# The decay and beta projection of a decoder step as an fp32 product on four column groups

## The chip, the cores and the metric

The kernel runs on one core of a Trainium2 chip. Time is device time in microseconds for one execution of the whole step. TensorE (PE in the profile) multiplies, VectorE (DVE), ScalarE (ACT) and GpSimd (POOL) work element by element, and SyncE (SP) issues the transfers.

## The reference, cut to what matters

One layer of a hybrid decoder is computed for a prompt of 512 tokens and for 8 x 4 sample tokens, 544 columns in all. The front of the layer is an input projection of a shifted and scaled x:

```
shift, scale, gate = split(silu(c) @ w_cond + b_cond, 3)
h = x * (1 + scale) + shift
[qa, ka, va, za, qkv_b, zb, a_b, b_b, g_a, g_b] = h @ w_in
```

Scale and shift have one value per feature for the whole prompt, and one per feature for each of the 8 sample rows. The change touches only a_b and b_b, 8 + 8 output columns of the 11280. From them come the decay exp(-exp(A_log) * softplus(a + dt_bias)) and beta = sigmoid(b) of the gated delta rule. Everything behind (attention, delta rule, gates, output projection, layer norm) stays as it is.

## The kernel before, in words

The 1024 input features are 8 k-tiles of 128. All activations lie with features on partitions, and a product has 544 columns in two halves of 272 (HF). Most products are made of three fp32r products of a high and a low part of each operand.

The kernel doesn't issue its instructions as it writes them down. `body` records them, and `schedule` works out one order for all engines: it plays the recording through with an estimated duration for each instruction, and on each engine takes the ready one with the smallest (rank, number), number being the place in the recording. Rank -1 goes first, the front's work has 0, the long stream of projections 9, the cache moves 30. The moves have due times spread over the planned run. PSUM banks are handed out in the recorded order within a rank: `pg` has three banks, `pp` and `pd` two, `pb` one. `rec.together()` keeps a group of instructions in one piece. `rec.either` lets the order choose ACT or DVE for an evacuation.

The front (up to about 52 us) needs c first. `cond_block(1, ...)` makes the scale and `cond_block(0, ...)` the shift, in blocks of one or two k-tiles, with products on four column groups: k-tile k goes to the output partitions 32 (k mod 4) and on, and a product with the 0/1 matrix `selc` then adds the four groups and turns the result. The blocks use a bank of `pg` or of `pb` in turn. To keep TensorE at work while the shift is not yet known, the first three projection tiles (`sums`, of W3) are computed from x1 = x * scale, in high and low parts `x1[0]` and `x1[1]`, and the part of the shift is added afterwards, as sh @ W3. The sums hold two banks each of `pp`, `pd` and `pg`. When the shift is there, h is written over x in `xT`, and `hhi` and `hlo` are its parts for the stream of projections.

The 16 columns of a_b and b_b lie behind the other 384 in W3. Before, their high and low parts stand side by side as the 32 columns of `hl`, and 2 halves x 8 k-tiles x 2 parts of x1 = 32 products give `abT`, with the high part in rows 0 to 15 and the low part in rows 16 to 31. Two ACT copies evacuate it. The shift's part is added to rows 0 to 15. In `gates()`, products with the 0/1 matrices `sel16` and `selab`, which repeat every 16 rows, add the rows that belong together and put tokens on partitions; decay and beta follow from there.

Of the kernel before, what the change touches and what calls it, by code (L numbers as in the profile page):

```python
# [11 lines left out]
F32 = mybir.dt.float32  # L12
F32R = mybir.dt.float32r
AF = mybir.ActivationFunctionType
# [6 lines left out]
KT = 8  # L21
SEQ = 512
# [3 lines left out]
NT = SEQ + NS  # L26
HF = NT // 2
# [223 lines left out]
class Recorder:  # L251
# [21 lines left out]
    def pool(self, make, name, bufs, side):  # L273
        return Pool(self, make, name, bufs, side)
# [506 lines left out]
def body(ctx, tc, io):  # L781
    rec = Recorder()
    pe, ve, se, ge, sp = rec.engines()
# [19 lines left out]
    def pg():  # L803
        return psg.tile([128, 512], F32, name="pg", tag="g")
# [4 lines left out]
    def pb_():  # L809
        return psb.tile([128, 512], F32, name="pb", tag="b")  # L810
# [14 lines left out]
    def C(name, where="early"):  # L825
        a, n = CCOLS[name]
        return tables[where][:, a:a + n]
# [13 lines left out]
    op = pool(octx, "opool", 9, "right")  # L841
# [41 lines left out]
    xT = fx.tile([128, KT, NT], F32, name="xT")  # L883
    W3 = fx.tile([128, KT, 400], F32, name="W3")
    sc = fx.tile([128, KT, 9], F32, name="sc")
    sh = fx.tile([128, KT, 32], F32, name="sh")
    early_ = op.tile([128, NT], F32, name="cg", tag="o")
    n = CONST[2].shape[1]
# [1 line left out]
    dta = early_[:, n:n + 68].rearrange("p (a b) -> p a b", b=34)  # L890
    shifts = early_[:, n + 68:n + 104].rearrange("p (a b) -> p a b", b=9)
    first = [op.tile([128, NT], F32, name="raw", tag="o") for _ in range(3)]
    abT = op.tile([128, NT], F32, name="abT", tag="o")[0:32]
    xs = xT[:, :, SEQ:].rearrange("p k (b t) -> p k b t", t=4)
    per_token = lambda t, k, n: t[:, k:k + n, 1:9, None].to_broadcast([128, n, 8, 4])
    cols_of = lambda n: slice(n * HF, (n + 1) * HF)
    with ExitStack() as fctx:
        fr = pool(fctx, "front", 1)
# [27 lines left out]
        sp.dma_start(bnw, io["b_norm_w"])  # L926
        ve.memset(cs, 0.0)
        ge.memset(sh, 0.0)
        th = fr.tile([128, KT, 9], F32, name="th")
        se.activation(th, cT, AF.Tanh, scale=0.5)  # L930
        ve.tensor_scalar(th, th, 0.5, 0.5, op0=OP.mult, op1=OP.add)
# [2 lines left out]
        def cond_block(part, at, m, other):  # L934

            ps, wc, w = pb_() if other else pg(), pieces[part, at], 128 * m
            idle = IDLE if (part, at) == (1, 0) else (0, 0, 0)
            rec.rank = -1

            def turn_over(n):  # L940
                for _ in range(n):
                    pe.matmul(ps[:, 384:512], ones, ones, start=True, stop=True)

            turn_over(idle[0])
            with rec.together():
                for k in range(KT):
                    q = k % 4
                    pe.matmul(ps[32 * q:32 * q + 32, 0:w].rearrange("p (a b) -> p a b", b=128), cs[:, k, :], wc[:, :, k, :],
                              start=(k < 4), stop=(k >= 4), tile_position=(0, 32 * q)).at = 9.9 * ((part, at) == (1, 1))
                turn_over(idle[1])  # L950
            Y = fr.tile([128, 256], F32, name="Y", bufs=2)
            ve.tensor_copy(Y[:, 0:w], ps[:, 0:w])
            pv = ps[:, 256:256 + 16 * m].rearrange("p (a b) -> p a b", b=16)
            with rec.together():
                for i in range(m):
                    pe.matmul(pv[:, i, 0:9], Y[:, 128 * i:128 * i + 128], C("selc", "first"), start=True, stop=True)
                turn_over(idle[2])
            rec.rank = 0
            return pv[:, :, 0:9], bT[:, 8 * part + at:8 * part + at + m, None].to_broadcast([128, m, 9])

        x1 = [fr.tile([128, KT, NT], F32R, name=f"x1{u}") for u in "hl"]
        sums = [[f()[:, :HF] for _ in range(2)] for f in (pp, pd, pg)]
        for b, (c, m) in enumerate(CHUNKS):
            pv, bias = cond_block(1, c, m, b % 2)
            kk = slice(c, c + m)
            ve.scalar_tensor_tensor(sc[:, kk], pv, 1.0, bias, op0=OP.add, op1=OP.add)
            for k in range(c, c + m):
                se.activation(x1[0][:, k, :SEQ], xT[:, k, :SEQ], AF.Copy, scale=sc[:, k, 0:1])
                if k == c:
                    ve.tensor_mul(xs[:, kk], xs[:, kk], per_token(sc, c, m))  # L970
                    se.activation(x1[0][:, kk, SEQ:], xT[:, kk, SEQ:], AF.Copy)
                    ve.tensor_sub(x1[1][:, kk, SEQ:], xT[:, kk, SEQ:], x1[0][:, kk, SEQ:].bitcast(F32))
                ve.scalar_tensor_tensor(x1[1][:, k, :SEQ], xT[:, k, :SEQ], sc[:, k, 0:1], x1[0][:, k, :SEQ].bitcast(F32),
                                        op0=OP.mult, op1=OP.subtract)
            hi, lo = (wsp.tile([128, D], F32R, name=n, tag=n)[:, 0:384 * m].rearrange("p (k c) -> p k c", k=m) for n in ("hi", "lo"))
            se.activation(hi, W3[:, kk, 0:384], AF.Copy)
            ve.tensor_sub(lo, W3[:, kk, 0:384], hi.bitcast(F32))
            for k in range(c, c + m):
                for t in range(3):
                    w, w_ = (x[:, k - c, 128 * t:128 * t + 128] for x in (hi, lo))  # L980
                    for n in range(2):
                        for a, x in ((w, 0), (w, 1), (w_, 0)):
                            pe.matmul(sums[t][n], a, x1[x][:, k, cols_of(n)], start=(k == 0 and a is w and x == 0),
                                      stop=(k == KT - 1 and a is w_))
        for t in range(3):
            for n in range(2):
                rec.either(first[t][:, cols_of(n)], sums[t][n])
        hl = fr.tile([128, KT, 32], F32R, name="hl")
        se.activation(hl[:, :, 0:16], W3[:, :, 384:400], AF.Copy)
        ve.tensor_sub(hl[:, :, 16:32], W3[:, :, 384:400], hl[:, :, 0:16].bitcast(F32))  # L990
        ps = [pg(), pg()]
        for n in range(2):
            for k in range(KT):
                for x in range(2):
                    pe.matmul(ps[n][0:32, :HF], hl[:, k], x1[x][:, k, cols_of(n)],
                              start=(k == 0 and x == 0), stop=(k == KT - 1 and x == 1))
        for n in range(2):
            se.activation(abT[:, cols_of(n)], ps[n][0:32, :HF], AF.Copy)
        for c, m in two_by_two:
            pv, bias = cond_block(0, c, m, c % 4)  # L1000
            kk = slice(c, c + m)
# [2 lines left out]
        ps, pv = pg(), pb_()  # L1004
        with rec.together():
            for k in range(KT):
                q = k % 4
                pe.matmul(ps[32 * q:32 * q + 32, 0:400], sh[:, k, :], W3[:, k, :], start=(k < 4), stop=(k >= 4),
                          tile_position=(0, 32 * q))
# [113 lines left out]
    def gates():  # L1123
# [14 lines left out]

        pa = pg()
        for c in range(4):  # L1140
            pe.matmul(pa[:, c * 16:c * 16 + 16], abT[:, c * 128:(c + 1) * 128], C("sel16", "g")[0:32], start=True, stop=True)
        sab = C("selab", "g").rearrange("p (a b) -> p a b", b=4)
        for h4 in range(4):
            pe.matmul(pa[32 * h4:32 * h4 + 32, 64:68], abT[:, SEQ:], sab[0:32, h4, :], start=True, stop=True)
        zero = op.tile([128, NT], F32, name="zero", tag="o")[0:16, 0:512]
        ge.memset(zero, 0.0)
        ab = d1.tile([128, 2, 34], F32, name="ab")
# [36 lines left out]
        g = d1.tile([128, 34], F32, name="g")  # L1184
# [356 lines left out]
    pairs = [{} for _ in range(4)]  # L1541
# [637 lines left out]
    rules = threads.add(chain(delta_rule), 0)  # L2179
    blocks = threads.add(chain(delta_blocks), 1)  # L2180
    threads.add(gates(), -2)
    threads.add(stream(57 + 4 + EARLY_B), 9)
    ap = pool(actx, "ap", 1)
# [125 lines left out]
    for k in range(0, KT, 2):  # L2309
        name = ("hi", "lo")[k // 4]  # L2310
# [69 lines left out]
    for tt, n in ((0, 0), (1, 0), (2, 0), (None, 0), (0, 1), (1, 1), (2, 1), (3, 0), (3, 1)):  # L2380
# [3 lines left out]
        q = r[tt]  # L2384
        step = 256 if n and tt == 3 else 512
        for c in range(512 * n, 512 * n + 512, step):
            po = product_out(tt, c, c + step)
            w = slice(c, c + step)
# [129 lines left out]
```

## Time and profile before

| | |
|---|---|
| median of 3 runs | 880.43 us (878.79 to 882.06) |
| profiled execution | 878.32 us, its span 876.5 us |
| granted TensorE clock, mean | 0.997 |
| busy: PE, DVE, ACT, POOL | 859.6, 643.1, 451.2, 69.6 us |
| chain that ended last | PE 84%, DVE 5%, ACT 4%, DMA 4% |
| DMA | 236.18 MB, mean 269 GB/s |

The span goes from the first to the last instruction of the core. PE counts matmuls, PEld weight loads, which run beside them. A row of the timeline has start and length in us, engine, line, operation, out<-in with the names of the tiles, the array's shape (rows*columns), the moving operand and the number of instructions merged; in brackets stands how long the engine was idle before it and what released it. All lines are L728, since one helper issues everything, so rows are told apart by tile names. An fp32 product is two records of the trace, an fp32r product one. The ends of matmuls are modelled; distances of starts are used below.

### The profile page before, as it was taken

To read this page: it belongs to the slowest core of one execution; us is meant where nothing else is said; L and a number is where in the kernel's file an instruction comes from. 1 tells how busy PE (TensorE), PEld (TensorE's weight loads), DVE (VectorE), ACT (ScalarE), POOL (GpSimd) and SP (SyncE) were. 2 spreads that over 40 slices of the span, in tenths; PEclk is the share of its full clock that TensorE was granted. 3 is DMA by queue.
4 is the path that set the end of the run, shared out by engine and by line. 5 is a ranking of instruction groups with operands and counts; after the bars stand their busy time and mean duration, and the time that the engine had idled before them with its cause. 6 is when DMAs were issued, how large, how long until landed. Compare 5 with 4: busy or idle time off the path is not lost.

```text
span 876.5 us, 20668 instructions
## 1 busy us (share of the span) xinstructions
PE 859.6 (98%) x8152; PEld 811.5 (93%) x8152; DVE 643.1 (73%) x1328; ACT 451.2 (51%) x1069; POOL 69.6 (8%) x167
## 2 busy tenths in 40 slices
PE   8999999999999999999999999999999999999996
PEld 7889999898999899999999998999999999999875
DVE  4775557565448999967999853556999699998547
ACT  3546656765546786447785446732442213234442
POOL 0120110110001110001020000011010000001000
PEclk9999999999999999999999999999999999999998
DMA  9976769666697886999877896469969899986984
GB/s 334 348 216 201 234 204 284 239 198 223 189 268 237 286 278 201 289 281 311 306 218 263 259 289 210 160 216 307 356 213 373 277 409 420 372 314 205 351 290 147
DMA packets 120493, 236.18 MB, mean 269 GB/s; under 512 B 49110, under 2 KB 76576, under 8 KB 117708
## 3 DMA queue, kind: packets, MB, share of 16 engines
q1 hardware_dynamic: 120396, 234.86, 80.0%
q8 instruction: 64, 1.05, 0.5%
q14 instruction: 33, 0.27, 0.1%
HBM read 218.53 MB, written 103.97 MB: 368 GB/s over the span
## 4 chain that ended last, share of the span: by engine, by line
PE 84%; DVE 5%; ACT 4%; DMA 4%; issue 1%; SPq 1%; POOL 0%; DVEq 0%; ACTq 0%
PE pp L728 64%; PE pg L728 9%; PE pd L728 8%; PE pb L728 4%; ACT L728 1%; DMA slab<-in_ks 1%; DMA dO<-orow 1%; DMA wc<-in_w_cb 1%; DMA wv<-dw 1%; DVE slab L728 1%; ACT sq L728 1%; DVE acc L728 1%; ACT hi L728 1%; DVE lo L728 1%; SPq L728 1%
## 5 line engine op out<-in xcount | busy, mean ns | idle before, releaser
L728 PE MATMUL pp<-hhi,hi 128*128 128x272 f32 x1360 | 397.6, 292 | 2.1 <-DVE zt L728 1.4
L728 PE MATMUL pp<-hhi,lo 128*128 128x272 f32 x1360 | 397.3, 292 | 0.0
L728 PE MATMUL pp<-hlo,hi 128*128 128x272 f32 x1360 | 395.7, 291 | 0.0
L728 PEld LDWEIGHTS pp<-hhi,hi 128*128 128x128 f32 x1360 | 256.4, 188 | 5.0 <-issue 1.8
L728 PEld LDWEIGHTS pp<-hhi,lo 128*128 128x128 f32 x1360 | 256.4, 188 | 2.1 <-issue 1.4
L728 PEld LDWEIGHTS pp<-hlo,hi 128*128 128x128 f32 x1360 | 256.3, 188 | 1.4 <-issue 0.4
L728 ACT ACTIVATE hi<-wt 128x1024 fp32r<-128x1024 f32 (+1 forms) x101 | 103.5, 1025 | 170.4 <-PE pp L728 141.2
L728 DVE TENSOR_TENSOR lo<-wt,hi 128x1024 fp32r<-128x1024 f32 (+1 forms) x101 | 118.9, 1177 | 71.6 <-ACT hi L728 71.3
L728 DVE SCALAR_TENSOR_TENSOR acc<-ext,cw,acc 128x568 f32<-128x568 f32 x72 | 58.0, 805 | 1.6 <-ACT acc L728 0.6
L728 DVE TENSOR_TENSOR slab<-slab 128x512 f32<-128x512 f32 (+1 forms) x66 | 42.9, 667 | 7.0 <-DMA slab<-in_vs 4.1
L728 DVE TENSOR_REDUCE slab<-slab 128x8 f32<-128x512 f32 (+2 forms) x66 | 42.7, 658 | 3.3 <-ACT slab L728 2.9
L728 ACT ACT_TABLE_LOAD x32 | 41.1, 1283 | 4.2 <-DMA dO<-orow 1.7
L728 ACT ACTIVATE zt<-pp 128x272 f32<-128x272 f32 x48 | 18.7, 389 | 37.7 <-PE pp L728 36.3
L728 PE MATMUL pp<-ybh,lo 128*128 128x272 f32 x128 | 36.9, 288 | 0.0
L728 PE MATMUL pp<-ybh,hi 128*128 128x272 f32 x128 | 36.9, 288 | 0.0
L728 ACT ACTIVATE P<-P,st 128x256 f32<-128x256 f32 (+1 forms) x64 | 31.1, 487 | 11.1 <-DVE st L728 11.0
L728 PE MATMUL pp<-ybl,hi 128*128 128x272 f32 x128 | 36.8, 287 | 0.0
L728 POOL COPY cx<-ext 128x3 f32<-128x3 f32 (+1 forms) x48 | 21.7, 480 | 151.4 <-ACT ext L728 149.9
L728 DVE CUSTOM_DVE_ANT_0 P<-pg,bias 128x256 f32<-128x256 f32 (+1 forms) x64 | 23.1, 403 | 13.2 <-PE pg L728 13.1
L728 PEld LDWEIGHTS pp<-ybh,hi 128*128 128x128 f32 x128 | 24.2, 189 | 0.2
L728 ACT ACTIVATE spare<-pp 128x272 f32<-128x272 f32 (+1 forms) x32 | 16.3, 509 | 15.5 <-PE pp L728 15.5
L728 PEld LDWEIGHTS pp<-ybh,lo 128*128 128x128 f32 x128 | 24.1, 189 | 0.1
(421 smaller groups left out, 1539.5 us busy)
## 6 DMA issues: line engine op xcount, KB each, us to landing
out_kv_s<-in_cache SPq DMA_DIRECT2D x144, 512.0 KB
wt<-in_w_in SPq DMA_DIRECT2D x85, 512.0 KB
out_kv_s<-in_cache SPq DMA_DIRECT2D x24, 496.0 KB
wc<-in_w_cb SPq DMA_DIRECT2D x16, 512.0 KB
slab<-in_ks SPq DMA_DIRECT2D x32, 256.0 KB
slab<-in_vs SPq DMA_DIRECT2D x32, 256.0 KB
kv<-in_ks SPq DMA_DIRECT2D x16, 512.0 KB
kv<-in_vs SPq DMA_DIRECT2D x16, 512.0 KB
```

The costliest lines, as they stand in the source:

```text
L728: getattr(real[x.engine], x.name)(*map(arg, x.args), **{k: arg(v) for k, v in x.kw.items()})
```

## The change

The products for a_b and b_b become plain fp32 products on four column groups. `wab` has the 16 weight columns and 16 columns of zeros for each k-tile. For the prompt, `wsc` is wab times the prompt's scale, and the moving operand is the raw x: 8 products of 512 columns, recorded with rank -1 and ahead of the evacuation of the sums. For the sample tokens, whose scales differ, 16 products of 32 columns take wab with the two parts of x1, read as fp32. `abT` now has 128 rows, four partial sums of 32 rows, and the selecting products run over 128 rows in place of 32, and add the four.

```diff
-    abT = op.tile([128, NT], F32, name="abT", tag="o")[0:32]
+    abT = op.tile([128, NT], F32, name="abT", tag="o")
...
+        wab, wsc = (fr.tile([128, KT, 32], F32, name=name) for name in ("wab", "wsc"))
+        ge.memset(wab, 0.0)
...
+        se.activation(wab[:, :, 0:16], W3[:, :, 384:400], AF.Copy)
+        ve.tensor_mul(wsc, wab, sc[:, :, 0:1].to_broadcast([128, KT, 32]))
+
+        def ab_product(out, pairs):
+            with rec.together():
+                for i, (w, x) in enumerate(pairs):
+                    q = 32 * (i % 4)
+                    pe.matmul(out[q:q + 32], w, x, start=(i < 4), stop=(i >= len(pairs) - 4), tile_position=(0, q))
+
+        ps = pg()
+        rec.rank = -1
+        ab_product(ps, [(wsc[:, k], xT[:, k, :SEQ]) for k in range(KT)])
+        se.activation(abT[:, :SEQ], ps, AF.Copy)
+        rec.rank = 0
         for t in range(3):
             for n in range(2):
                 rec.either(first[t][:, cols_of(n)], sums[t][n])
-        hl = fr.tile([128, KT, 32], F32R, name="hl")
-        se.activation(hl[:, :, 0:16], W3[:, :, 384:400], AF.Copy)
-        ve.tensor_sub(hl[:, :, 16:32], W3[:, :, 384:400], hl[:, :, 0:16].bitcast(F32))
-        ps = [pg(), pg()]
-        for n in range(2):
-            for k in range(KT):
-                for x in range(2):
-                    pe.matmul(ps[n][0:32, :HF], hl[:, k], x1[x][:, k, cols_of(n)],
-                              start=(k == 0 and x == 0), stop=(k == KT - 1 and x == 1))
-        for n in range(2):
-            se.activation(abT[:, cols_of(n)], ps[n][0:32, :HF], AF.Copy)
+        ps = pg()[:, 0:32]
+        ab_product(ps, [(wab[:, k], x1[x][:, k, SEQ:].bitcast(F32)) for k in range(KT) for x in range(2)])
+        se.activation(abT[:, SEQ:], ps, AF.Copy)
...
-            pe.matmul(pa[:, c * 16:c * 16 + 16], abT[:, c * 128:(c + 1) * 128], C("sel16", "g")[0:32], start=True, stop=True)
+            pe.matmul(pa[:, c * 16:c * 16 + 16], abT[:, c * 128:(c + 1) * 128], C("sel16", "g"), start=True, stop=True)
...
-            pe.matmul(pa[32 * h4:32 * h4 + 32, 64:68], abT[:, SEQ:], sab[0:32, h4, :], start=True, stop=True)
+            pe.matmul(pa[32 * h4:32 * h4 + 32, 64:68], abT[:, SEQ:], sab[:, h4, :], start=True, stop=True)
```

## Prediction

> **What bounds the kernel now.** First the page: its span, then the busy share of each engine.
>
> ```profile
> span 876.5 us, 20668 instructions
> PE 859.6 (98%) x8152; PEld 811.5 (93%) x8152; DVE 643.1 (73%) x1328; ACT 451.2 (51%) x1069; POOL 69.6 (8%) x167
> ```
>
> TensorE is busy nearly all the time, but a busy TensorE need not be one that sets the end, so the next view is the table by stretches (length, then busy time and instruction count of each engine, granted clock, DMA share).
>
> ```profile
> 0.00:13.00 13.00, 9.99 (x84) 8.74 (x85) 4.67 (x18) 4.28 (x8) 0.52 (x5) 1.00 0.82 280
> 13.00:30.00 17.00, 16.95 (x153) 14.65 (x153) 9.85 (x23) 6.97 (x13) 0.00 (x0) 1.00 1.03 412
> 30.00:39.00 9.00, 9.00 (x95) 6.87 (x94) 5.81 (x15) 4.32 (x9) 1.95 (x3) 1.00 1.01 398
> 39.00:48.60 9.60, 9.60 (x90) 6.87 (x89) 6.75 (x15) 5.79 (x12) 4.74 (x10) 1.00 0.74 170
> 76.00:200.00 124.00, 123.97 (x1222) 117.94 (x1222) 75.04 (x179) 77.10 (x193) 14.32 (x43) 1.00 0.73 237
> 200.00:850.00 650.00, 644.52 (x6192) 614.48 (x6191) 501.04 (x979) 326.37 (x770) 45.03 (x93) 1.00 0.83 278
> ```
>
> The reader is to see three things. From 13 to 48.6 us, where the whole change lies, TensorE has 0.05 us without work, at a granted clock of 1.00. From 76 to 200 us it has 0.03 us without work, so whatever TensorE is spared before 48 us is handed on. In the 650 us after that it lacks 5.48 us, the only stretch in which small waits could swallow or return anything. So the change is worth the TensorE time that it takes away or adds, as long as TensorE always has something else to run in its place.
>
> **What is removed.** The 32 products of x1 with the narrow weights. Rows of the tile hl (duration ns, first and last start), and the first and the last of twelve such products in a row on the timeline:
>
> ```profile
> L728 PE MATMUL pg<-x1h,hl x16: 282/287/289, 40.2 to 47.6; 128*32 128x272 f32 x16
> L728 PE MATMUL pg<-x1l,hl x16: 282/287/314, 40.3 to 47.7; 128*32 128x272 f32 x16
> L728 DVE TENSOR_TENSOR hl<-W,hl x1: 280/280/280, 27.7 to 27.7; 128x128 fp32r<-128x128 f32 x1
> ```
>
> ```profile
> 42.04 0.29 PE L728 MATMUL pg<-x1h,hl 128*32 128x272 f32 x1
> 43.42 0.28 PE L728 MATMUL pg<-x1l,hl 128*32 128x272 f32 x1
> ```
>
> The 287 ns are a latency; what a product costs is the distance of starts, (43.42 - 42.04)/11 = 0.1255 us. So 32 x 0.1255 = 4.02 us of TensorE goes.
>
> **What is added: the prompt part.** Eight fp32 products of 512 columns on four column groups. The trace has this shape: the rows of wg, 8 products in 16 records. For what a change of tiling costs I show a block of 256 columns and the ordinary products behind it.
>
> ```profile
> 156.31 0.29 PE L728 MATMUL pp<-hhi,hi 128*128 128x272 f32 x1
> 156.53 1.92 PE L728 MATMUL pd<-wg,cs 128*32 128x512 f32 x16
> 158.38 0.66 PE L728 MATMUL pg<-cst,P 128*128 128x128 f32 x4
> ```
>
> ```profile
> 24.69 1.07 PE L728 MATMUL pg<-wc,cs 128*32 128x256 f32 x16
> 25.69 0.39 PE L728 MATMUL pd<-x1h,hi 128*128 128x272 f32 x1
> 25.92 0.28 PE L728 MATMUL pd<-x1l,hi 128*128 128x272 f32 x1
> ```
>
> From the block's start to the next work: 158.38 - 156.53 = 1.85 us. On the way in, 156.53 - 156.31 less one step of 0.1255 is 0.09 us; on the way out, 25.92 - 25.69 less a step is 0.10 us. Sum 2.04 us. The same count for 256 columns, 25.69 - 24.69 + 0.19, is 1.19 us: nearly proportional, as it should be if the four groups run beside each other.
>
> **The sample part.** Sixteen fp32 products of 32 columns, 32 records. The nearest row has the same shape, 24 products in 48 records, behind another block of column groups:
>
> ```profile
> 393.91 0.66 PE L728 MATMUL pg<-ks,Qz 128*32 128x32 f32 x48
> 394.50 0.39 PE L728 MATMUL pp<-hlo,hi 128*128 128x272 f32 x1
> ```
>
> (394.50 - 393.91)/48 = 12.3 ns a record, so 32 take 0.39 us, and with a turn in and out 0.58 us, which I take. The lower end is 0.39 us, if it runs beside another block. The upper end goes by small products that share nothing:
>
> ```profile
> 47.82 0.87 PE L728 MATMUL pb<-sel,Y 128*128 128x9 f32 x8
> 48.62 0.39 PE L728 MATMUL pp<-hhi,hi 128*128 128x272 f32 x1
> ```
>
> that is 0.80/8 = 0.10 us a record and 3.2 us for 32. The 48-record row has shape and tiling of the new product, so I stay near it.
>
> Here a rule speaks against the change: the Trainium skill (TensorEngine Tiling, Instruction Overhead) gives each matmul some 60 cycles, whatever its width. By it, at 2.4 GHz, the 32 records would take an estimated 0.8 us instead of 0.39, and the gain below would be 1.1 us instead of 1.5. The 12.3 ns of this trace do not agree with that where four groups take turns.
>
> **The selecting products.** Before, 16 records with 32 rows:
>
> ```profile
> 51.42 1.23 PE L728 MATMUL pg<-cg,abT 32*128 32x16 f32 x16
> 52.58 0.39 PE L728 MATMUL pp<-hhi,hi 128*128 128x272 f32 x1
> ```
>
> They take 1.16 us and a turn in and out, 1.35 us. After, the first 8 records have the shape of those at 47.82 (0.80 us, no turn in), the other 8 are narrow (8 x 0.0123 = 0.10 us) with two turns (0.19 us) and a little for the change between: 1.1 to 1.35 us. I take a gain of 0.1 us; ends 0.25 us gained and 0.2 us lost, since the second half is in no row.
>
> **The other engines.** Durations of the parts that change:
>
> ```profile
> L728 ACT ACTIVATE abT<-pg x2: 387/387/387, 43.5 to 48.0; 32x272 f32<-32x272 f32 x2
> ```
>
> ```profile
> L728 ACT ACTIVATE R<-pg 128x512 f32<-128x512 f32 x2 | 1.2, 600 | 0.8 <-PE pg L728 0.8
> ```
>
> ```profile
> L728 DVE TENSOR_TENSOR R<-Z,R 128x256 f32<-128x256 f32 x2 | 0.8, 424 | 0.0
> ```
>
> ```profile
> L728 POOL MEMSET sh<- 128x256 f32 x1 | 0.3, 312 | 0.3 <-POOLq L2491 0.3
> ```
>
> ACT: two evacuations of 0.387 us become one of 0.60 us and a small one (estimate 0.2 us); the copy of the 16 weight columns stays. DVE: the subtraction of 0.28 us becomes the scaling wsc of 0.42 us, 0.14 us more. POOL: one more memset of 0.31 us in the first stretch, where it works 0.52 of 13 us. No DMA is added, removed or moved, and SP waits for nothing new.
>
> ```profile
> 27.57 0.17 DVE L728 SCALAR_TENSOR_TENSOR sc<-pg,bT 128x18 f32<-128x18 f32 x1
> ...
> 28.53 0.75 DVE L728 SCALAR_TENSOR_TENSOR x1l<-xT,sc,x1h 128x512 fp32r<-128x512 f32 x1 [0.46 <-ACT x1h L728]
> ...
> 31.23 0.42 DVE L728 COPY Y<-pg 128x256 f32<-128x256 f32 x1 [1.15 <-PE pg L728]
> 32.69 0.18 DVE L728 TENSOR_TENSOR sh<-pg,bT 128x18 f32<-128x18 f32 x1 [1.04 <-PE pg L728]
> ```
>
> wsc needs the last scale, ready at 27.74 us, and DVE then idles 0.46 us before 28.53 and 1.15 us before 31.23: the 0.42 us fit, cost nothing, and would only move the prompt product later if they did not. So the product runs at 28.6 to 30.6 us at the earliest, 30.5 to 32.5 at the latest, with the sums on TensorE around it.
>
> **The wait that this adds.** The prompt product takes the third pg bank, the one that the shift blocks of pg also use, and is ahead of them in their order (both have rank -1).
>
> ```profile
> 30.09 1.07 PE L728 MATMUL pg<-wc,cs 128*32 128x256 f32 x16
> ```
>
> ```profile
> 35.89 1.07 PE L728 MATMUL pg<-wc,cs 128*32 128x256 f32 x16
> ```
>
> ```profile
> 38.95 0.29 PE L728 MATMUL pg<-x1h,lo 128*128 128x272 f32 x1
> 39.07 0.29 PE L728 MATMUL pp<-hhi,hi 128*128 128x272 f32 x1
> ```
>
> ```profile
> 45.84 1.36 DVE L728 TENSOR_TENSOR hlo<-xT,hhi 128x544 fp32r<-128x544 f32 x2 [0.72 <-ACT hhi L728]
> ```
>
> With product and evacuation over (0.6 us and a hand-over), the first shift block starts at 31.3 to 33.2 us instead of 30.09. Behind it stand its Y copy, its sh (32.69 before) and the h of two k-tiles. The next pg block, at 35.89, needs the bank that this frees 2.8 us after its start, at 34.1 to 36.0 us: there the delay has died out. TensorE does not notice, since the sums, pushed back by 2.04 us, end at 41.0 instead of 39 us. From 41.0 until the last hlo (45.84 + 1.36 = 47.2 us) it needs 6.2 us of other work. It has the 36 products of the first job with k below 6 (36 x 0.1255 = 4.5 us), the last shift block (1.2 us), its selection (0.4 us), the sample product (0.6 us) and the sh product (between the 256 and the 512 column blocks, estimate 1.6 us): 8.3 us. The cover is 2.1 us more than is needed.
>
> **The sum.** 4.02 - 2.04 - 0.58 + 0.10 = 1.50 us less. Span 876.5 - 1.5 = 875.0 us; the profiled execution took 878.32 us, 1.8 us around its span, so 876.8 us for it. It was 2.1 us below the median of the three runs, 880.43 us, so for the median I say 878.9 us. The ends of the terms give 1.50 + 0.19 + 0.15 = 1.8 us gained, and 1.50 - 2.62 - 0.30 = 1.4 us lost.
>
> **The rivals.**
> (a) *TensorE starves between 41 and 50 us, slower.* If h of the last k-tiles slips by more than the 2.1 us of cover, TensorE waits; past 2.1 + 1.5 = 3.6 us of slip the kernel is slower than before, and 0.5% (4.4 us) needs 8 us. For it speaks the block at 30.09, which must wait; against it that the delay has gone at 35.89, by the order of the banks. A slip of 5 us would give 881.8 us.
> (b) *The order of the rest changes.* The order of all instructions is worked out from estimated times, with cache moves due at fixed times; a front shorter by 1.5 us shifts everything against them. The stretch from 200 to 850 us lacks 5.48 us of TensorE work: this bounds what a lucky order returns, and I take as much for an unlucky one. That is 873.4 to 884.4 us. Against a big effect: the 39 to 200 us part has almost no idle time to change.
> (c) *The change does not save what it says:* the groups take turns at full length. Then eight products of 512 columns would take four times 1.85 us, 7.4 us, and with the small ones at 3.2 us the kernel would be some 7 us slower, 887 us. The 1.85 us of the wg row, with 16 records of 592 ns in it, speak against it.
>
> **How the numbers follow.** Forecast as summed, with an order that moves it by less than 2 us: 0.74. Rival (b) beyond that, lucky 0.12, unlucky 0.06; (a) 0.06; (c) 0.02. The likeliest case gives 878.9 us. A difference below 0.5%, 4.4 us, can hardly be told from none, for the three runs lie 3.3 us apart. Faster by more than that, below 876.0 us, takes most of lucky (b) and a low median: 0.11. Slower by more, above 884.8 us: (c), the far end of (a) and (b), 0.05. Within: 0.84. The range for 8 in 10 goes from 875.4 us (the sum with 3.5 us of lucky order) to 882.0 us (rival (a) at 5 us, or the lost end of the terms).
>
> **What would show it.** Right: a group of 16 records of 512 columns, mean about 590 ns, start to next work 1.85 us, between 28 and 33 us; 32 records of 32 columns in about 0.4 us; no record of x1 by 272 columns with 32 output columns; one abT evacuation of 512; the products with hhi without a break from 41 us. The later work should stand about 1.5 us earlier. Wrong: a first shift block after 34 us, TensorE idle between 41 and 50 us (rival a), a different idle sum between 200 and 850 us (rival b), or a prompt product of over 2.2 us (rival c).

## The result: 0.7% slower, by a wait 190 us behind the change

The changed kernel takes 886.61 us in the median of 7 runs (884.89 to 889.28), beside 880.8 us (877.24 to 884.61, 7 runs) of the kernel before on the same chip: ratio 1.007, 95% interval 1.0052 to 1.0087. Forecast was 878.9 us, in a range up to 882.0. The profiled execution took 887.46 us, and its span is 885.7 us, 9.2 us longer than before.

The page of the changed kernel, span, engines and granted clock in 40 slices:

```profile
span 885.7 us, 20707 instructions
PE 861.0 (97%) x8168; PEld 813.2 (92%) x8168; DVE 642.0 (72%) x1327; ACT 454.2 (51%) x1072; POOL 68.3 (8%) x168
PEclk9999999999899999999999999999999999999999
```

TensorE is without work for 885.7 - 861.0 = 24.7 us; before it was 876.5 - 859.6 = 16.9. And the clock falls in the eleventh slice, near 225 us, where the kernel before has a 9. The front is not there, as its own rows on the timeline show:

```profile
30.48 0.29 PE L728 MATMUL pd<-x1h,hi 128*128 128x272 f32 x1
30.69 1.92 PE L728 MATMUL pg<-xT,wsc 128*32 128x512 f32 x16
32.55 0.39 PE L728 MATMUL pp<-x1l,hi 128*128 128x272 f32 x1
...
33.62 1.07 PE L728 MATMUL pg<-wc,cs 128*32 128x256 f32 x16
...
37.82 1.07 PE L728 MATMUL pg<-wc,cs 128*32 128x256 f32 x16
...
43.34 0.19 PE L728 MATMUL pg<-x1h,wab 128*32 128x32 f32 x1
...
43.75 0.39 PE L728 MATMUL pp<-hhi,lo 128*128 128x272 f32 x1
...
53.04 0.96 PE L728 MATMUL pg<-cg,abT 128*128 128x16 f32 x8
53.85 0.37 PE L728 MATMUL pp<-hlo,hi 128*128 128x272 f32 x1
...
55.02 0.25 PE L728 MATMUL pg<-cg,abT 128*32 128x4 f32 x8
55.20 0.39 PE L728 MATMUL pp<-hhi,hi 128*128 128x272 f32 x1
```

The prompt product costs 32.55 - 30.69 = 1.86 us and its turns, the 32 sample records 43.75 - 43.34 = 0.41 us, the selection 0.81 and 0.18 us. And the later work does stand earlier. The same product of the stream with hhi and hlo, the 401st, in the kernel before and in the changed one:

```profile
105.60 0.29 PE L728 MATMUL pp<-hlo,hi 128*128 128x272 f32 x1
```

```profile
104.73 0.29 PE L728 MATMUL pp<-hlo,hi 128*128 128x272 f32 x1
```

That is 0.87 us earlier, although up to 76 us TensorE was without work for 3.85 us here and for 3.21 us before. The two make 1.5 us, what the front was to save. The table by stretches says where the idle time went. The first fence below is of the kernel before, for one stretch that was not shown; the second of the changed kernel:

```profile
200.00:859.00 659.00, 653.52 (x6233) 621.82 (x6232) 507.59 (x993) 331.85 (x782) 45.03 (x93) 1.00 0.83 278
```

```profile
13.00:30.00 17.00, 15.57 (x145) 13.65 (x138) 9.75 (x22) 6.97 (x13) 0.00 (x0) 1.00 1.03 409
39.00:48.60 9.60, 9.46 (x112) 8.16 (x116) 8.28 (x19) 6.10 (x15) 4.45 (x7) 1.00 0.81 185
200.00:859.00 659.00, 646.45 (x6187) 617.22 (x6186) 498.64 (x970) 327.20 (x766) 40.05 (x93) 0.99 0.81 275
```

From 200 to 859 us the idle time is 12.55 us, 7.1 more than the 5.48 before, and the clock is no longer full. Where, the list of TensorE's waits of the changed kernel tells (total, times, longest):

```profile
PE pg L728 <- ACT spare L728: 3.7, 1, 3.7
PE pg L728 <- DVE o L728: 2.8, 1, 2.8
PE pg L728 <- issue: 1.8, 1, 1.8
PE pb L728 <- DMA wc<-in_w_cb: 1.7, 2, 1.4
```

The 1.4 us for `wc`, at 17 us, are weights coming from memory late in this execution; the first 13 us lack 0.7 us less than before in return. In the kernel before the waits are shorter; the longest, and the two for `NTs`, of which more below:

```profile
PE pb L728 <- DVE NTs L728: 1.3, 2, 0.8
PE pg L728 <- DVE ones L728: 1.1, 1, 1.1
```

The timeline at the longest one, changed kernel:

```profile
221.87 1.14 DVE L728 SCALAR_TENSOR_TENSOR NTs<-cr,cum,cst 128x128 f32<-128x128 f32 x4 [5.30 <-DMA dO<-orow]
223.20 0.63 ACT L728 ACTIVATE NTs<-NTs 128x512 f32<-128x512 f32 x1
223.74 0.38 ACT L728 ACTIVATE spare<-pp 128x272 f32<-128x272 f32 x1
224.17 0.69 PE L728 MATMUL pg<-cst,spare 128*128 128x128 f32 x2 [3.65 <-ACT spare L728]
```

It reads upward. TensorE lacks 3.65 us for `spare`, an evacuation (the copy of a product out of PSUM) on ACT; that stood on ACT behind the exponential of `NTs`; that waited for DVE's decay matrix; and DVE waited 5.30 us for a store, dO<-orow, because `NTs` is handed the buffer in which `orow`, the output rows of the delta rule, lay. The transfers as SP issued them, changed kernel, and then the same two and the same DVE instruction in the kernel before:

```profile
213.25 0.23 SPq L728 DMA_DIRECT2D dg<-grow  x1
213.59 0.37 SPq L728 DMA_DIRECT2D dO<-orow  x1
```

```profile
211.69 0.28 SPq L728 DMA_DIRECT2D dg<-grow  x1
...
222.66 0.38 SPq L728 DMA_DIRECT2D dO<-orow  x1
...
225.71 1.14 DVE L728 SCALAR_TENSOR_TENSOR NTs<-cr,cum,cst 128x128 f32<-128x128 f32 x4 [2.26 <-DMA dO<-orow]
```

Before, DVE goes on 225.71 - 222.66 = 3.05 us after the store of `orow` is issued; after, 221.87 - 213.59 = 8.28 us. The store is the same; the new thing is that dg<-grow, 73 rows of 2 KB, is issued 0.34 us ahead of it and not 11 us. The records of single DMA engines tell the rest: of the 16 parts of dO, 15 were through between 215.48 and 217.38 us, the sixteenth at 221.85. From 213.5 us on, 201 packets of 2 KB were moved, the 128 rows of dO and the 73 of `grow`; from 217.5 us until the last at 221.44 they start one every 80 ns and take 84 ns each, so one engine alone was still at work on them. And dg<-grow itself ends in a single part, at 221.21 us, where dO has 16. All 73 rows of `grow` had gone to that engine, with the last sixteenth of dO behind them. The Trainium skill (DMA: Bandwidth & Descriptors, Why a DMA increments its semaphore by 16 and not by 1) says that a transfer issued from SP is spread over the largest number of engines up to 16 that divides the outer dimension of both its sides; 73 is a prime, which leaves one engine, and the records agree.

The last piece is the clock. Stretches of the changed kernel:

```profile
213.60:221.90 8.30, 6.92 (x51) 6.35 (x49) 1.67 (x5) 3.15 (x15) 0.00 (x0) 1.00 0.72 231
221.90:226.00 4.10, 1.83 (x8) 1.74 (x9) 2.44 (x9) 2.71 (x4) 0.00 (x0) 0.69 0.14 32
226.00:231.00 5.00, 5.00 (x24) 4.73 (x23) 2.77 (x5) 1.47 (x4) 0.00 (x0) 0.57 0.52 159
```

The granted clock is one half for 6.8 us from 223.5 us on, while the work is there. So the wait costs 3.65 us and about 3 us more. The same follows the wait of 2.8 us for `o` at 793 us, with 3.4 us at half clock from 796.9 us on; the changed kernel's stretch there has a granted clock of 0.84:

```profile
790.00:800.00 10.00, 7.19 (x60) 6.24 (x59) 7.75 (x17) 1.50 (x6) 0.00 (x0) 0.84 0.76 252
```

### The profile page after: what moved, and what is told of

Read it like the earlier page. It is cut to its first block, busy times and chain, and to the rows that moved or that the text cites. A ratio compares the mean times of both kernels' runs of the same rounds, so it can differ in the third digit from the quotient of the medians.

```text
span 885.7 us, 20707 instructions
## 1 busy us (share of the span) xinstructions
PE 861.0 (97%) x8168; PEld 813.2 (92%) x8168; DVE 642.0 (72%) x1327; ACT 454.2 (51%) x1072; POOL 68.3 (8%) x168
## 4 chain that ended last, share of the span: by engine, by line
PE 86%; DVE 5%; DMA 3%; ACT 2%; issue 2%; SPq 0%; POOL 0%; DVEq 0%; ACTq 0%
PE pp L728 65%; PE pg L728 9%; PE pd L728 8%; PE pb L728 4%; DMA wc<-in_w_cb 2%; DVE acc L728 1%; DVE lo L728 1%; DMA dO<-orow 1%; DMA rbo<-dO 1%; ACT L728 1%; DVE slab L728 0%; DVE od L728 0%; ACT sq L728 0%; DVE zt L728 0%; DVE NTs L728 0%
## 5 line engine op out<-in xcount | busy, mean ns | idle before, releaser
L728 POOL COPY cx<-ext 128x3 f32<-128x3 f32 (+1 forms) x48 | 19.6, 436 | 147.7 <-ACT ext L728 145.4
```

What stands on the lines that cost most here:

```text
L728: getattr(real[x.engine], x.name)(*map(arg, x.args), **{k: arg(v) for k, v in x.kw.items()})
```

## The experiments

The theory at the outset: the front saves what was forecast, and the order that is worked out anew for everything behind it loses some 8 us, most of it in the chain above. The main rival: the front itself is dear, by its rank or by its waits. Ratios are to the kernel before, measured on the same chip as each experiment.

**E1 and E2, the front and the order taken apart.** Both recordings are planned; the kernel follows its own plan up to 50 us, and from there the other kernel's order.

```diff
+def splice(rec, other, until):
+    head = [... what rec's own order starts before `until` ...]
+    ... then every other instruction in other's order, on other's engine
...
         rec.schedule()
+        other.schedule()
+        splice(rec, other, 50.0)
```

E1 is the new front with the old order, E2 the old front with the new order.

> The changed kernel, but from 50 us of the plan on the instructions stand in the order of the kernel before (the front in its own order). Order theory: what the change lost came from the order that the schedule worked out anew for the rest, and the product itself spares 1.5 us of TensorE: 880.8 - 1.5 = 879.3 us, ratio to before 0.998, and no wait of TensorE of 3 us or more at 210 to 230 us. Front theory: the product itself, its bank or its longer moving operand costs the time, whatever the order of the rest: 886 us, ratio 1.006.

> The kernel before with its 32 fp32r products, but from 50 us of the plan on in the order of the changed kernel. Order theory: it has the loss without the gain, 886.6 + 1.5 = 888 us, ratio 1.008, and a wait of TensorE of 3 to 4 us near 220 us with the clock at half for about 7 us behind it. Front theory: 880.8 us, ratio 1.000.

Measured: E1 879.16 us (877.61 to 882.42), ratio 0.999 (0.9975 to 1.0006). E2 889.57 us (886.45 to 892.91), ratio 1.0107 (1.0085 to 1.013). The loss goes with the order; the old front in the new order has it in full. TensorE's waits of E2 show the same two, and a third:

```profile
PE pg L730 <- ACT spare L730: 3.7, 1, 3.7
PE pg L730 <- DVE o L730: 2.8, 1, 2.8
PE pp L730 <- issue: 2.3, 1, 2.3
```

The third, at 397 us, has 6.8 us at half clock behind it, and the changed kernel doesn't have it; so the distance between E2 and the changed kernel is not a measure of the front.

**P1 and P2, another order with no instruction changed.** The kernel before, with the fixed due times of cache moves and gates 1.5 us later (P1) or earlier (P2).

```diff
-MOVES = (48.0, 850.0)
-GATES = (110.0, 200.0)
+MOVES = (49.5, 851.5)      # P2: (46.5, 848.5)
+GATES = (111.5, 201.5)     # P2: (108.5, 198.5)
```

> The kernel before, no instruction changed; only the due times of the cache moves and of the gate rows are 1.5 us later, so that the schedule works out another order, about as far off as the change puts it. Order theory: the time moves by some us either way, anywhere from 876 to 888 us, with other waits of TensorE than before. Front theory: an order as good as the first, 880.8 us within 1.5 us.

> The kernel before with all due times 1.5 us earlier, no instruction changed; the counterpart of P1, where they were 1.5 us later. Theory (every shift of the front against the fixed due times draws another order, and what it costs is a matter of which waits it happens to draw): another order with other idle places; the time is not foretold, 878 to 890 us, and goes with TensorE's longest waits: above 884 us only if a wait of over 2.5 us is there. Rival (P1 lost because later cache moves are worse in themselves): earlier ones cost nothing or gain, 877 to 881 us, whatever the waits.

Measured: P1 887.17 us (885.69 to 887.79), ratio 1.0076 (1.006 to 1.0091); P2 885.29 us (881.05 to 889.33), ratio 1.0054 (1.0032 to 1.0077). Moving the plan by 1.5 us either way costs 5 to 7 us. P2 missed a detail of its expectation: its longest wait is 2.3 us, below the 2.5 us that I had set. In neither run does TensorE wait over 0.9 us at once for `NTs`: their loss lies in other waits, of which the longest are for `o`, 2.8 us in P1 and 2.3 us in P2.

**E3, E4 and E5, the chain at 220 us cut in three places,** each in the changed kernel. E3 lets `orow` share the buffer of `vr`, so that `NTs` does not wait for the store. E4 keeps the buffer and moves the second store of `grow` behind the cache moves that follow; it is then issued 4.4 us after dO. E5 keeps order and buffer and cuts the stores of `grow` in two.

```diff
 E3
+        orow.base.alias = vr.base
 E4
...
+        item = o.pop(dg)
...
+        o.insert(at + 1, item)
 E5
...
+                    for p in (slice(0, 64), slice(64, 73)):
+                        real[x.engine].dma_start(*(arg(v[p]) for v in x.args))
```

> The changed kernel in its own order throughout; only the output rows of a delta head (orow) are written over vr, which is dead by then, and no longer share buffers with NTs, so that the next NTs need not wait for the store dO<-orow. If the wait near 220 us comes from that shared buffer: the 3.7 us wait of TensorE and the half clock of 6.8 us behind it (3.4 us) go, 886.6 - 7 = 879.6 us, ratio 0.999. If NTs waits for something else there, the wait stays and so does the time, 886.6 us. If only the wait goes but other waits take its place: between, 882 to 885 us.

> The changed kernel in its own order; only the second store dg<-grow (73 rows of 2 KB), which stands 0.34 us ahead of the store dO<-orow on SP, is issued after the next two cache moves instead. If those 73 rows keep one DMA engine busy for 6 us and the last sixteenth of dO waits for it: dO lands 2 to 3 us after its issue instead of 8.2, the 3.7 us wait of TensorE near 220 us and the half clock behind it go, 886.6 - 7 = 879.6 us, ratio 0.999. Rival: dO is slow because of the 512 KB cache moves around it; then nothing changes, 886.6 us.

> The changed kernel in its own order, the stores dg<-grow in place; each is issued as two, of 64 and of 9 rows. If it is the number of rows, 73, that puts all of a store on one DMA engine, 64 rows spread over 16 and dO is late by 1 us at most: 879.6 us, ratio 0.999. If the rows go to one engine whatever their number, or the cache moves are what delays dO: 886.6 us.

Measured: E3 878.39 us (875.64 to 882.5), ratio 0.9989 (0.9972 to 1.0005); E4 878.76 us (877.02 to 882.31), 0.9984 (0.9963 to 1.0006); E5 879.16 us (876.58 to 884.79), 0.999 (0.9967 to 1.0012). Each alone takes back the whole loss. In E5 order, waits and buffers are those of the changed kernel, and the two pieces still go ahead of dO; rows of E5's timeline:

```profile
212.70 1.04 SPq L730 DMA_DIRECT2D dg<-grow  x2
213.85 0.34 SPq L732 DMA_DIRECT2D dO<-orow  x1
217.01 1.14 DVE L732 SCALAR_TENSOR_TENSOR NTs<-cr,cum,cst 128x128 f32<-128x128 f32 x4 [0.98 <-DMA dO<-orow]
```

DVE goes on 3.16 us after the issue of dO in place of 8.28. The pieces of 64 and 9 rows have landed at 214.99 and 215.14 us, 2.3 and 1.9 us after their issue, where the 73 rows took 8.0 us. So it is the 73 rows on one engine, not the store as such.

**E8, the reverse:** the kernel before, with that one store moved to the place directly ahead of dO.

```diff
...
+        item = o.pop(dg)
...
+        o.insert(at, item)        # at: the next store dO<-orow
```

> The kernel before with one store moved and nothing else: the second dg<-grow (73 rows), issued at 211.69 us and 11 us ahead of dO<-orow, is now issued immediately ahead of it. Theory (the 73 rows go to one DMA engine, and the last sixteenth of dO waits behind them): dO, which landed some 3 us after its issue at 222.66 us, lands about 7 to 8 us after it; NTs comes 4 to 5 us later than 225.7 us, TensorE idles 4 to 5 us there and runs at half clock behind it, in all 7 to 9 us more: 887 to 889 us. Rival one (the place of the store is harmless, and the order of the changed kernel lost its time by its sum of many things): within 1 us of before, 879 to 881 us. Rival two (the wait comes, but the clock does not follow): 4 to 5 us more, 884 to 885 us.

Measured: 885.64 us (885.14 to 888.35), ratio 1.0062 (1.0038 to 1.0086), 5.4 us more. Rows of E8's timeline, then its stretch around the wait:

```profile
220.26 0.30 SPq L728 DMA_DIRECT2D dg<-grow  x1
220.65 0.36 SPq L728 DMA_DIRECT2D dO<-orow  x1
...
229.07 1.14 DVE L728 SCALAR_TENSOR_TENSOR NTs<-cr,cum,cst 128x128 f32<-128x128 f32 x4 [6.19 <-DMA dO<-orow]
...
232.24 1.38 PE L728 MATMUL pb<-KQ 128*128 128x256 f32 x4 [4.43 <-DVE NTs L728]
```

```profile
220.00:240.00 20.00, 15.57 (x106) 14.90 (x105) 7.34 (x19) 8.76 (x24) 0.00 (x0) 0.91 0.49 162
```

dO took 229.07 - 220.65 = 8.4 us, about as foretold, and TensorE waits 4.43 us. `NTs` comes 3.4 us later than before and not 4 to 5, for dO is issued 2.0 us earlier than before (the case of E7 below shows what had held it up). The median is 1.4 us below the 887 to 889 us: the clock was at half for 3.4 us here and not 6.8, although the wait is longer. One store, moved by 8.6 us, does most of what the change did.

**E3b and E6, orow's buffer in the old order:** E3's edit in the kernel before (E3b), and in E1 (E6).

> New front, the order of the kernel before from 50 us on, and orow written over vr: both things that helped. Order theory: 879.2 us less what is left of the waits for dO in that order (DVE waits 3.1 us for it, TensorE 0.9 us behind NTs): 878 us, ratio 0.9975. If the shared buffer cost nothing in this order: 879.2 us, ratio 0.999.

> The kernel before with the tile orow in the buffer of vr, so that NTs no longer waits for the store of orow. Theory: in this order nothing but 0.8 us of TensorE's idle time hangs on that buffer, so the time stays within 1 us of before, 879 to 881 us, and what E6 gained against before (878.4 us) is the four column groups' own 1.5 us. Rival: the buffer itself is worth 2 us here too: 878 us or less.

Measured: E6 878.39 us (875.51 to 880.95), ratio 0.997 (0.9953 to 0.9987); E3b 878.21 us (876.7 to 880.85), ratio 0.9976 (0.9962 to 0.9989). My expectation of E3b fell, and its rival stands: the buffer is worth 2.1 us in the old order too, though the wait on `NTs` that it removes was 1.3 us in all. So the time of E6 shows nothing of the new product, all the more as E1 and E6 have a wait of their own where the two orders are joined. E1's timeline and stretch there:

```profile
52.38 1.24 PE L730 MATMUL pg<-cg,abT 128*128 128x16 f32 x16 [0.86 <-DVE abT L730]
```

```profile
50.00:60.00 10.00, 9.14 (x68) 8.84 (x68) 7.72 (x35) 5.04 (x11) 1.81 (x7) 0.83 0.50 155
```

Behind it the clock is at half for 3.4 us.

**E9, E10 and E11.** E9 is E6 with E5's cut. E10 is E1 and E11 is E9 with the orders joined at 58 us, behind the selection (`splice(rec, other, 58.0)`).

> E6 (the new front in the old order, with orow in the buffer of vr) and both stores of grow cut into 64 and 9 rows. Theory: with NTs free of the store, nothing on TensorE waits for the 73 rows any more, so the cut gives nothing further: 878 to 879 us, as E6. Rival: the rows on one DMA engine hold up other transfers as well, such as the weights for which TensorE waits 1.8 us in E6: 876 to 877 us.

> E1 (the new front, then the old order) with the two orders joined at 58 us of the plan instead of 50 us, so behind the selecting products. Theory (the front saves its 1.5 us, and E1 lost it again at the joint: 1.1 us of TensorE's idle time before pg<-cg,abT and half of 3.4 us at half clock): no gap and no half clock between 50 and 60 us, the products with hhi stand 1.2 to 1.8 us earlier than before at 84 us, and the time is 877 to 879 us beside 880 us of before, ratio 0.996 to 0.9985. Rival (what the front saves is swallowed by the old order's own waits, joint or not): as E1, 0.999 or above.

> E9 (E1's join, orow in the buffer of vr, the stores of grow cut into 64 and 9 rows) with the joint at 58 us. Theory: the joint's 2.8 us go, 873.5 to 875.5 us, ratio 0.993 to 0.995, and faster than both kernels by more than the interval. Rival (as for E10): as E9, 876 to 877 us, ratio 0.996.

Measured: E9 876.39 us (874.57 to 881.05), ratio 0.9959 (0.9943 to 0.9975); E10 878.39 us (875.65 to 883.19), 0.9981 (0.9962 to 1.0); E11 876.19 us (874.59 to 878.21), 0.9951 (0.9928 to 0.9974). E10's time came as the theory said, 1.7 us below before, though its interval just reaches 1; the way there did not. The products with hhi were to stand 1.2 to 1.8 us earlier than before, and the 401st of the stream starts at 106.58 us, 0.98 us later than the 105.60 us of before. Up to there TensorE lacked 2.1 us more, so the front is 1.1 us shorter, and a new wait takes more than that. What E10's profiled execution gains, it gains behind 200 us, where TensorE lacks 2.81 us up to 859 us beside 5.48; no run says why. The new joint only moved the wait, as the same stretch of E10 and then of E11 shows:

```profile
60.00:70.00 10.00, 8.60 (x70) 7.77 (x69) 9.64 (x29) 7.00 (x21) 1.22 (x6) 1.00 0.23 66
```

```profile
60.00:70.00 10.00, 8.60 (x57) 7.51 (x56) 8.96 (x31) 5.78 (x18) 1.22 (x6) 0.83 0.25 77
```

Both lack 1.4 us there, and E11 has 3.4 us at half clock behind it as well; so E11 missed its 873.5 to 875.5 us. Both E9 and E11 are faster than both kernels, by 0.4 to 0.5% than the one before. That the cut adds to E6 is not shown: the intervals of E6 and E9 overlap.

**E7, the changed kernel with P1's due times.** It was to draw an order without the 73 rows directly ahead of dO.

> The changed kernel, all its instructions, with due times 1.5 us later, and so one more order. Order theory: not the 886.6 us again but some other time between 874 and 890 us; without a store dg just ahead of a store dO, below 884 us. Front theory: 886.6 us within 1.5 us.

Measured: 886.86 us (885.21 to 889.53), ratio 1.0068 (1.0047 to 1.0089). A miss. The pair is 12 us apart in it, and yet, on its timeline:

```profile
217.45 5.87 SPq L728 DMA_DIRECT2D out_kv_p<-spare  x4
224.20 0.52 SPq L728 DMA_DIRECT2D out_kv_s<-in_cache  x1
224.82 0.53 SPq L728 DMA_DIRECT2D dO<-orow  x1
...
229.11 1.14 DVE L728 SCALAR_TENSOR_TENSOR NTs<-cr,cum,cst 128x128 f32<-128x128 f32 x4 [6.50 <-DMA dO<-orow]
...
232.18 2.08 PE L728 MATMUL pb<-KQ 128*128 128x256 f32 x4 [3.34 <-DVE NTs L728]
```

The same buffer is late in another way: dO stands on SP's queue behind four stores of `spare`, as before, and a cache copy, is issued 2.2 us later than before, and DVE goes on 4.3 us behind the issue in place of 3.05. SP's own waits in E7, from 205 to 232 us, say what held the queue:

```profile
SPq L728 <- DMA dg<-grow: 3.2, 1, 3.2
```

The fourth store of `spare` counts its landing on the semaphore that dg<-grow uses, and so SP didn't issue it before the 73 rows had landed, at 222.99 us, 10.7 us after their issue; the fourth store goes at 223.00. In the kernel before, SP waits 2.3 us for the same store. So the 73 rows are at work here too, by holding up SP's queue and not dO's last sixteenth: the 16 parts of dO land together, from 228.49 to 229.01 us. Why that takes 4.2 us from the issue is not shown, nor was the store cut in this order. E7 also has two further waits, 1.7 us at 407 us and 2.1 us at 614 us, each with 3.4 us at half clock. The weak place is `NTs` waiting for a store; the 73 rows hit it in two ways.

## Why the prediction was wrong

**The terms of the sum held.** Prompt product: 1.86 us and turns of 0.09 and 0.10 us, 2.05 in place of 2.04. Sample product: 0.41 us with no turn in, for it ran directly behind a shift block: the lower end (0.39) rather than the 0.58 that I took, and 12.8 ns a record. The 0.8 us that the prediction worked out by the rule of the Trainium skill (TensorEngine Tiling, Instruction Overhead) did not appear. The prediction counted the 60 cycles for each of the 32 records; counted for each of the 16 products, at 2.4 GHz, they give an estimate of 0.40 us, and 0.60 us for the 24 products that took 0.59 us. Read so, the traces do not speak against the rule. Selection: 0.81 and 0.18 us where I had 0.80 and 0.10. That makes the gain about 1.7 us in place of 1.50. The 401st product of the stream, 0.87 us earlier with 0.64 us more idle time, gives 1.5 us; the same count in E3, E4, E5, E7 and E10 gives 0.8 to 1.7 us. E10's 1.7 us in the median (interval 0.0 to 3.3) are near this figure by luck, as far as its profiled execution shows.

**The wait that it adds** was underestimated, at no cost. The prompt product came at the late end of its window (30.69), the first shift block at 33.62 instead of by 33.2, the next at 37.82 instead of by 36.0, so the delay had not died out there. The cover of 2.1 us was enough: TensorE lacks 0.14 us from 39.0 to 48.6. Rival (a) did not come, nor did (c).

**Rival (b) is the step that failed,** in its bound and in its chance. It named the mechanism: the order of the rest is worked out from estimated times against fixed due times, and a shorter front shifts it. Three things in it were wrong, and one further up in the prediction.
- "I take as much for an unlucky one": 5.48 us, the idle time of one order, does bound what a luckier order can return. It bounds no loss. The changed kernel has 12.55 us there, 7.1 more.
- It left out the clock. A TensorE wait of some microseconds is followed by 3.4 or 6.8 us at half clock, in all 10.2 us of them here beside none ahead of the kernel's end before; at nearly half the pace that is 4 to 5 us, which no sum of idle times contains.
- "No DMA is added, removed or moved" holds for the edit and not for the order that is worked out from it: dg<-grow and dO<-orow, 11 us apart before, stand 0.34 us apart, and this one pair brought the 3.65 us wait and the 6.8 us at half clock behind it.
- The chances, 0.12 for lucky and 0.06 for unlucky, were the wrong way round. P1, P2, E7 and the change itself are four redrawn orders, and all lie between 885.3 and 887.2 us; the order of the kernel before, with 5.48 us idle, is the exception. Four draws are few, but none came near the forecast. That little idle time was the evidence that there was little to win and much to lose, and I read it as "almost no idle time to change".

The account of the span: 7.8 us more idle time in all and 4 to 5 us of slow clock, less 1.7 us of the front, would be 10 to 11 us; measured are 9.2. About 1 to 2 us of that are not assigned.

## What to carry to other kernels

Where one planner orders everything, price an edit as its own terms plus a redraw of the order: shift the planner's times a little with no other change and time that, for it gives the spread before the edit is judged (here 5 to 7 us against an edit of 1.7). Here the bound engine was idle for less than 1% behind 200 us, and all four redrawn orders were worse; in such a kernel I would give the unlucky side most of the chance. And look for buffers that are released by a store: cutting the store of 73 rows into 64 and 9, or giving its neighbour another buffer, each took back the whole loss.

## What the hardware showed that I had not expected

- A store of 73 rows of 2 KB, 146 KB, is through 8.0 us after its issue (8.8 us in the kernel before, 10.7 in E7), on one DMA engine at some 80 ns a row, and the last sixteenth of a 256 KB store issued 0.34 us behind it lands 4.5 us after the other fifteen.
- The granted clock falls to a half after shorter gaps than I would have thought, and not in proportion to them. The Trainium skill (TensorE: Matmul & The Clock Gate, Part 1) gives an idle window of about 3.4 us for it. The lengths at half clock, 3.4 or 6.8 us, are one and two of these, but the gaps do not keep to it: 3.65 us was followed by 6.8 us (changed kernel), 4.43 us by 3.4 (E8), 0.86 us by 3.4 (E1), and 1.4 us by 3.4 in E11 and by none in E10. Part of it is where a gap lies. In every trace the stretches at full clock from the first rise of the clock to each drop, and from one drop to the next, are whole multiples of 3.413 us (in the changed kernel 218.45 us, which is 64 of them, 566.61 us, 166, and 81.92 us, 24), so the clock changes on a fixed grid. The wait of 2.80 us for `o` lies in one interval of this grid in E5, 783.36 to 786.78 us, in which TensorE is busy for 0.25, and 3.4 us at half clock follow; in E3 it lies across two, which are busy for 0.56 and 0.62, and the clock stays full. This does not account for the shortest gaps: the interval with the 0.86 us of E1 is busy for 0.75, that of E11 for 0.59 and that of E10 for 0.62. What else counts there is open.
- Sixteen fp32 products of 32 columns on four column groups cost 0.41 us, 12.8 ns a record with the time to the next work in it (their starts alone lie 9 ns apart), and directly behind another block of column groups there is no turn to pay.
